# Column order of the moving operand in the fp32r products of a two-block forward pass

## The chip, the cores and the metric

The kernel runs on one core of a Trainium2 chip. The metric is the device time of one execution in microseconds (us), as the median of several runs. Engines are named as the profile names them: PE is the matrix engine (PEld its weight loads), DVE the vector engine, ACT the scalar engine, POOL and SP the two others.

## The reference

The program is the forward pass of two transformer-like blocks over 512 tokens of width 1,024, all in float32. The first block has a layer norm, a wide input projection, a spatial gating branch, a gated delta rule branch, a merge of the two, and a mixture of 32 experts (two chosen per token). The second block prepends 16 meta tokens and has attention with rotary positions, a gated linear recurrence, a merge, and a gated feed-forward part.

```
h = layer_norm(x)
proj = h @ w_in + b_in                               # all inputs of both mixers
merged = sigmoid(gate_a) * (y_a @ w_pa) + sigmoid(gate_b) * (y_b @ w_pb)
h = layer_norm(alpha * h + merged @ w_o)
h = layer_norm(alpha * h + moe(h))                   # 32 experts, top 2
proj = rmsnorm(h) @ w_in_2                           # q, k, v, rnn input, gates
h = h + (g_attn * attention + g_rnn * rnn) @ w_out
h = h + (silu(g) * u) @ w_ffn_out                    # g, u = rmsnorm(h) @ w_ffn_in
```

## The kernel before

Most products are made from split operands. `split` (L137) writes a float32 tile as two tiles of type fp32r: the high part is a copy on ACT, the low part is the rest, a subtraction on DVE. `mm3` (L162 to L166) then adds three matmuls into one PSUM bank: high by high (L164), high by low (L165), low by high (L166). Its second and third arguments are the stationary pair, loaded before each matmul; its fourth and fifth are the moving pair, whose columns run through the array.

The dense products come in two forms. `dense_fm` (L168) computes 128 output features for all 512 tokens: the stationary tiles are 128 columns of weights, the moving tiles are the tokens, 512 columns, with 8 steps over the width, so 24 matmuls into one bank. The projections of the first block (`gmlp`, `delta`), the gates of the second (`gates`) and the first half of the feed-forward part (`ffn`) use it; ACT, and in `ffn` also DVE, takes the bank out. `dense_tm`, `dense_tok` and `tm_step` compute 128 tokens by 512 features: the tokens are stationary and 512 columns of weights move. Weights come as float32 chunks by DMA on SP's queue (`wraw_load`, L156) and are split in `wchunk` (L148), in `split_w` (L307), `split_kv` (L1643) and `split_q` (L1739).

Five further places have moving fp32r tiles: `merge_b` (L810) moves 256 columns, two runs of 128; `rnn_x` (L1952) moves 264; the attention scores (L2053) move 264 columns of keys and the attention output (L2087) 512 columns of probabilities; the experts' results go back to the tokens in `add` (L1287 and L1288), 512 columns, and `add_res` (L1293) adds that bank to the residual on DVE. `combine` (L1295) does this 8 times for each of the 16 pairs of experts. `moe` gives the PSUM pool `psA` four buffers (L1158).

The expert products themselves (L1231 and L1261) are plain float32. Each is issued as two passes, and two experts stand side by side, 64 output rows each, in the two halves of the array. Rows of tokens for the experts are picked by fp32r products of 256 columns (L1194, L1195). Four small DVE operations are named below for their read patterns: in the routing of tokens L1031 multiplies the 32 expert logits of a token, taken from the four groups by turns (a step of 8), and L1004 forms 128 products in order; in `delta` L531 copies 32 columns of a PSUM bank and L582 reads 32 at an inner step of 32. Expert weights are loaded ahead in 1 MB chunks (`ahead`, L1123) on SP's queue.

The order of instructions on PE, and in some stretches on DVE and ACT too, is written out by hand (`manual_schedule` in `layer_in`, `moe`, `norm_kvq`, `block2` and `mix_out`); elsewhere a scheduler puts them in the order of the program.

Of the kernel before, what the change touches and what calls it, by code (L numbers as in the profile page):

```python
# [44 lines left out]
def weave(chain, others):  # L45

    for f in others:
        next(chain, None)
        f()
    for _ in chain:  # L50
        pass


class Net:
# [93 lines left out]
    def wchunk(self, wap, r0, nk, c0, ncol):  # L148

        raw = self.wraw_load(wap, r0, nk, c0, ncol)  # L150
        hi = self.whl.tile([128, nk, ncol], FR, name="whi")
        lo = self.whl.tile([128, nk, ncol], FR, name="wlo")
        self.split(hi, lo, raw)
        return hi, lo

# [124 lines left out]
    def layer_in(self, ctx, gp, v, hT):  # L280
# [24 lines left out]
        lo, ws = {}, []  # L305

        def split_w(n):  # L307
            hl = [self.whl.tile([128, 2, 512], FR, name=m) for m in ("whi", "wlo")]
            ws.append(hl)
            self.act(hl[0], raws[n], AF.Copy)  # L310
            return lambda: V.tensor_tensor(hl[1], raws[n], hl[0].bitcast(FT), OP.subtract)

        def stats(t):
            one = slice(t, t + 1)
# [115 lines left out]
    def gmlp(self, ctx, gp, v, hT):  # L430
        nc, I = self.nc, self.I
        w_in = I["w_in"][0]
        tp = self.pool(ctx, "gt", 2)
        lg = self.bcast(gp, I["gm_ln_g"], D, "gm_lg")
        lb = self.bcast(gp, I["gm_ln_b"], D, "gm_lb")
        bs = self.bcast(gp, I["gm_b_s"], D, "gm_bs")

        wT = gp.tile([128, NK, 128], FT, name="gm_wT")
        ws = gp.tile([128, NK, 128], FT, name="gm_ws")
        nc.sync.dma_start(ws, I["gm_w_s"][0].rearrange("g t s -> t g s"))  # L440
        for g0 in range(0, NK, 4):
# [12 lines left out]
        for g in range(NK):  # L454
            pu = self.dense_fm(w_in, g * 128, hT)
            u = tp.tile([128, S], FT, name="gm_u")
            self.act(u, pu, AF.Gelu, bias=self.vec[:, g:g + 1])
# [12 lines left out]
        for m in range(NK):  # L470
            pa = tp.tile([128, S], FT, name="gm_pa")
            self.act(pa, self.dense_fm(w_pa, m * 128, (yhi, ylo)), AF.Copy)
            nc.scalar.dma_start(self.pa_d[m], pa)

    def delta(self, dp, hT, vb):
# [13 lines left out]
        with ExitStack() as c:  # L489
# [166 lines left out]
        with ExitStack() as c:  # L656
# [119 lines left out]
            def gate(dst, c0, b0, func):  # L776

                for m in range(NK):
                    z = tp.tile([128, S], FT, name="zs")
                    self.act(z, self.dense_fm(w_in, c0 + m * 128, hT), func, bias=self.vec[:, b0 + m:b0 + m + 1])  # L780
                    nc.scalar.dma_start(dst[m], z)

            gate(self.zt_d, 5120, 40, AF.Silu)
# [13 lines left out]
    def merge_b(self, tp, yb, mhi, mlo):  # L797

        nc, I = self.nc, self.I
        for m in range(NK):  # L800
# [6 lines left out]
            pb = self.psA.tile([128, 512], FT, name="psA")  # L807
            for i, (yhi, ylo) in enumerate(yb):
                for k in range(NK):
                    self.mm3(pb[:, i * 256:(i + 1) * 256], hi[:, k, :], lo[:, k, :], yhi[:, :, k, :], ylo[:, :, k, :],  # L810
                             k == 0, k == NK - 1)
            nc.vector.tensor_tensor(sb, pb, sb, OP.mult)
# [342 lines left out]
    def moe(self, pctx):  # L1155
# [3 lines left out]
        with ExitStack() as ctx:  # L1159
# [121 lines left out]
            def add(part, t, half):  # L1281
# [2 lines left out]
                ps = self.psA.tile([128, 512], FT, name="psA")  # L1284
                cs = slice(half * 512, (half + 1) * 512)
                a = PT[:M, TOKS[t]]
                nc.tensor.matmul(ps, a, yhi[:M, cs], start=True, stop=False)  # L1287
                nc.tensor.matmul(ps, a, ylo[:M, cs], start=False, stop=True)  # L1288
                return lambda: add_res(ps, t, half)

            def add_res(ps, t, half):
                x = self.res[:, t, half * 512:(half + 1) * 512]
                nc.vector.tensor_tensor(x, x, ps, OP.add)  # L1293

            def combine(part, between=lambda: None):  # L1295
                for t in range(NT):
# [318 lines left out]
    def norm_kvq(self, c, h, xT, kv, gp):  # L1615
# [25 lines left out]
        xn, pk, ws, wq = {}, {}, [], []  # L1641

        def split_kv(n):  # L1643
            hl = [self.whl.tile([128, 2, 512], FR, name=m) for m in ("whi", "wlo")]
            ws.append(hl)
            self.act(hl[0], raws[n], AF.Copy)
            return lambda: V.tensor_tensor(hl[1], raws[n], hl[0].bitcast(FT), OP.subtract)

        def stats(t):

# [88 lines left out]
        def split_q(n):  # L1739
            raw = self.wraw_load(w_in, 2 * n * 128, 2, 0, 512)  # L1740
            out = []
            for j in range(2):
                hl = [gp.tile([128, 1, 512], FR, name=f"{m}{2 * n + j}") for m in ("ga", "rn")]
                r = raw[:, j:j + 1, :]
                self.act(hl[0], r, AF.Copy)
                out.append(lambda hl=hl, r=r: V.tensor_tensor(hl[1], r, hl[0].bitcast(FT), OP.subtract))
                wq.append(hl)
            return out

# [185 lines left out]
    def rnn_x(self, p, n, vec, xT):  # L1935
# [12 lines left out]
        for j in range(2):  # L1948
            js = slice(j * H, (j + 1) * H)
            ps = self.psA.tile([128, 512], FT, name="psA")  # L1950
            for k in range(NK):
                self.mm3(ps[:, :H], hi[:, k, :], lo[:, k, :], nhi[:, k, js], nlo[:, k, js], k == 0, k == NK - 1)  # L1952
            self.act(xr[:, 2 + j * H:2 + (j + 1) * H], ps[:, :H], AF.Copy)
# [27 lines left out]
    def gates(self, p, n, xT, rn, ga):  # L1981
# [7 lines left out]
        self.act(ga[n], ps, AF.Tanh, scale=0.5)  # L1989
        yield  # L1990
        g = rn[n]
        self.act(g, self.dense_fm(w_in, 4608 + n * 128, real), AF.Tanh, scale=0.5)
        yield
        ps = self.dense_fm(w_in, 2560 + n * 128, real)
        x = p.tile([128, S], FT, name="grx")
        self.act(x, ps, AF.Copy)
        y = p.tile([128, S], FT, name="gry")
        self.act(y, ps, AF.Square)
# [37 lines left out]
    def attention(self, tp, h, kv, rn, ga, gp, mix):  # L2036
# [11 lines left out]
        def weights(t):  # L2048
            tok = TOKS[t]
            ps = self.psD.tile([128, 2, 512], FT, name="psD")  # L2050
            for j in range(2):
                js = slice(j * H, (j + 1) * H)
                self.mm3(ps[:, j, :H], q[0][:, tok], q[1][:, tok], khi[:, g, js], klo[:, g, js], True, True)  # L2053
            m = tp.tile([128, 1], FT, name="m", bufs=4)
            nc.vector.tensor_reduce(m, ps[:, :, :H], AX.XY, OP.max)
            nc.vector.scalar_tensor_tensor(m, m, -1.0, qs[:, t, h:h + 1], op0=OP.mult, op1=OP.mult)
            pr = tp.tile([128, 2, H], FT, name="pr", bufs=3)
            s = tp.tile([128, 1], FT, name="s", bufs=4)
            self.act(pr, ps[:, :, :H], AF.Exp, bias=m, scale=qs[:, t, h:h + 1], accum_out=s)
# [24 lines left out]
        vs = slice(g * 128, (g + 1) * 128)  # L2084
        for b in range(NT + 1):
            M = 128 if b else META
            self.mm3(po, vhi[:M, b, vs], vlo[:M, b, vs], Phi[:M, b, :], Plo[:M, b, :], b == 0, b == NT)  # L2087
        o = tp.tile([128, S], FT, name="ao")
        nc.vector.scalar_tensor_tensor(o, ga[h], 1.0, po, op0=OP.add, op1=OP.mult)
        yield  # L2090
        nc.vector.tensor_tensor(o, o, rn[h], OP.add)
        self.dbg("mix%d" % h, o)
# [57 lines left out]
    def ffn(self, ctx, h, hT, first):  # L2150
# [3 lines left out]
        fp = self.pool(ctx, "ffp", side="right")  # L2154
        f = (fp.tile([128, NF, S], FR, name="f_hi"), fp.tile([128, NF, S], FR, name="f_lo"))
        for m in range(NF):
            pg = self.dense_fm(w_i, m * 128, hT) if m else first[0]
            g = tp.tile([128, S], FT, name="fg")
            self.act(g, pg, AF.Silu)
            pu = self.dense_fm(w_i, (NF + m) * 128, hT) if m else first[1]  # L2160
            nc.vector.tensor_tensor(g, g, pu, OP.mult)
# [99 lines left out]
```

## Time and profile before

| what | value |
|---|---|
| median of 3 runs | 2016.44 us (2016.29 to 2017.75) |
| the profiled execution | 2013.71 us |
| its span | 2011.2 us |
| PE busy | 1931.3 us (96%), 9,833 matmuls |
| PEld, DVE, ACT busy | 1402.6 us, 1002.4 us, 700.1 us |
| moved by DMA | 362.22 MB |

The span is that of the instructions of one profiled execution; its time is 2.5 us longer, and the median of the runs is 2.7 us above that time. A matmul's listed duration has a modelled end and overlaps the next matmul; the distance from one start to the next is what a matmul takes in a row of them. A line number can be that of a helper: L68 is every ACT operation, L140 every low part, L164 to L166 every split product.

### The profile page before, as it was taken

To read this page: it belongs to the slowest core of one execution; us is meant where nothing else is said; L and a number is where in the kernel's file an instruction comes from. 1 tells how busy PE (TensorE), PEld (TensorE's weight loads), DVE (VectorE), ACT (ScalarE), POOL (GpSimd) and SP (SyncE) were. 2 spreads that over 40 slices of the span, in tenths; PEclk is the share of its full clock that TensorE was granted. 3 is DMA by queue.
4 is the path that set the end of the run, shared out by engine and by line. 5 is a ranking of instruction groups with operands and counts; after the bars stand their busy time and mean duration, and the time that the engine had idled before them with its cause. 6 is when DMAs were issued, how large, how long until landed. Compare 5 with 4: busy or idle time off the path is not lost.

```text
span 2011.2 us, 24965 instructions
## 1 busy us (share of the span) xinstructions
PE 1931.3 (96%) x9833; PEld 1402.6 (70%) x9833; DVE 1002.4 (50%) x1908; ACT 700.1 (35%) x1220; POOL 3.1 (0%) x12
## 2 busy tenths in 40 slices
PE   7999999879999899999999989999999999999999
PEld 5787668668888754554435536888888788888887
DVE  6833667744555822322223249557878753333222
ACT  5232434323332321111101116357677632222211
POOL 0000000000000000000000000000000000000000
PEclk9999999989999899999999998999999999999999
DMA  8423433464378499996999983432221333333231
GB/s 257 104 84 97 115 71 85 132 146 85 91 247 291 155 349 402 409 409 269 405 409 410 407 309 130 126 90 79 79 59 53 99 106 94 93 95 93 93 115 62
DMA packets 309015, 362.22 MB, mean 180 GB/s; under 512 B 29921, under 2 KB 196354, under 8 KB 308770
## 3 DMA queue, kind: packets, MB, share of 16 engines
q1 hardware_dynamic: 301986, 345.94, 51.8%
q10 hardware_dynamic: 6912, 14.68, 1.9%
q8 instruction: 78, 1.28, 0.3%
q14 instruction: 39, 0.32, 0.0%
HBM read 340.64 MB, written 19.94 MB: 179 GB/s over the span
## 4 chain that ended last, share of the span: by engine, by line
PE 45%; DMA 4%; DVE 2%; ACT 1%; issue 0%; SPq 0%; ACTq 0%; DVEq 0%
PE psA L165 10%; PE psA L164 10%; PE psA L166 10%; PE psB L1231 3%; DMA mwt<-in_w 3%; PE psB L1261 2%; PE psD L1975 1%; PE psA L1287 1%; PE psA L1288 1%; PE psD L164 1%; PE psB L2073 1%; PE psA L1195 1%; PE psA L1194 1%; PE psB L164 1%; PE psD L166 0%; PE psD L165 0%
## 5 line engine op out<-in xcount | busy, mean ns | idle before, releaser
L68 ACT ACTIVATE whi<-raw 128x1024 fp32r<-128x1024 f32 (+1 forms) x203 | 213.4, 1055 | 530.5 <-PE psA L165 300.7
L140 DVE TENSOR_TENSOR wlo<-raw,whi 128x1024 fp32r<-128x1024 f32 (+1 forms) x195 | 236.7, 1215 | 293.6 <-ACT whi L68 276.5
L1231 PE MATMUL psB<-mwt,XT 128*64 128x512 f32 x1008 | 226.1, 597 | 3.0 <-DVEq L1345 2.1
L166 PE MATMUL psA<-hT_hi,wlo 128*128 128x512 f32 (+1 forms) x456 | 184.7, 405 | 12.9 <-DVE wlo L140 12.9
L164 PE MATMUL psA<-hT_hi,whi 128*128 128x512 f32 (+1 forms) x456 | 185.7, 407 | 0.9 <-ACT whi L68 0.9
L165 PE MATMUL psA<-hT_lo,whi 128*128 128x512 f32 (+1 forms) x456 | 185.6, 407 | 0.0
L1231 PEld LDWEIGHTS psB<-mwt,XT 128*64 128x64 f32 x1008 | 73.3, 138 | 142.3 <-issue 136.4
L165 PE MATMUL psA<-hn_lo,whi 128*128 128x512 f32 (+1 forms) x368 | 141.8, 385 | 0.3 <-DVE hn_lo L2125 0.3
L164 PE MATMUL psA<-hn_hi,whi 128*128 128x512 f32 (+1 forms) x368 | 141.9, 386 | 0.2 <-ACT hn_hi L68 0.2
L166 PE MATMUL psA<-hn_hi,wlo 128*128 128x512 f32 (+1 forms) x368 | 141.7, 385 | 0.0
L1293 DVE TENSOR_TENSOR res<-res,psA 128x512 f32<-128x512 f32 x128 | 79.5, 681 | 103.0 <-PE psA L1288 103.0
L1237 DVE TENSOR_TENSOR sl<-sl,psB 128x512 f32<-128x512 f32 x16 | 11.0, 688 | 233.7 <-PE psB L1231 233.7
L1261 PE MATMUL psB<-mwt,hbT 128*64 128x512 f32 x480 | 110.2, 593 | 5.2 <-DMA mwt<-in_w 5.2
L164 PE MATMUL psA<-xn_hi,whi 128*128 128x512 f32 (+1 forms) x320 | 113.1, 353 | 0.4 <-ACT qx L68 0.4
L165 PE MATMUL psA<-xn_lo,whi 128*128 128x512 f32 (+1 forms) x320 | 112.3, 351 | 0.0
L166 PE MATMUL psA<-xn_hi,wlo 128*128 128x512 f32 (+1 forms) x320 | 111.9, 350 | 0.0
L166 PEld LDWEIGHTS psA<-hT_hi,wlo 128*128 128x128 f32 (+1 forms) x456 | 86.6, 190 | 35.3 <-DVE wlo L140 13.9
L165 PEld LDWEIGHTS psA<-hT_lo,whi 128*128 128x128 f32 (+1 forms) x456 | 86.5, 190 | 26.9 <-issue 7.5
L164 PEld LDWEIGHTS psA<-hT_hi,whi 128*128 128x128 f32 (+1 forms) x456 | 86.8, 190 | 24.5 <-issue 3.4
L1261 PEld LDWEIGHTS psB<-mwt,hbT 128*64 128x64 f32 x480 | 35.9, 137 | 76.5 <-issue 63.7
L68 ACT ACTIVATE hbT<-psA 128x512 f32<-128x512 f32 x16 | 9.6, 598 | 213.3 <-PE psA L1245 213.3
L165 PEld LDWEIGHTS psA<-hn_lo,whi 128*128 128x128 f32 x368 | 69.2, 188 | 15.7 <-DVE hn_lo L2125 0.5
(570 smaller groups left out, 3714.1 us busy)
## 6 DMA issues: line engine op xcount, KB each, us to landing
mwt<-in_w SPq DMA_DIRECT2D x188, 1024.0 KB, 13.6
raw<-in_w_in SPq DMA_DIRECT2D x108, 512.0 KB, 7.1
raw<-in_w_ffn_in SPq DMA_DIRECT2D x44, 512.0 KB, 3.9
raw<-in_w_ffn_out SPq DMA_DIRECT2D x22, 512.0 KB, 3.6
raw<-in_w_pa SPq DMA_DIRECT2D x8, 512.0 KB, 3.7
raw<-in_w_pb SPq DMA_DIRECT2D x8, 512.0 KB, 5.7
raw<-in_w_o SPq DMA_DIRECT2D x8, 512.0 KB, 6.7
raw<-in_w_out SPq DMA_DIRECT2D x8, 512.0 KB, 3.6
```

What stands on the lines that cost most here:

```text
L68: ins = self.nc.scalar.activation(out, in_, func, **kw)
L140: self.nc.vector.tensor_tensor(lo, x, hi.bitcast(FT), OP.subtract)
L164: nc.tensor.matmul(out, whi, xhi, start=first, stop=False)
L165: nc.tensor.matmul(out, whi, xlo, start=False, stop=False)
L166: nc.tensor.matmul(out, wlo, xhi, start=False, stop=last)
L1194: nc.tensor.matmul(ps[:, :n], h1hi[:, k, TOKS[t]], P[:, t, :], start=(t == 0), stop=False)
L1195: nc.tensor.matmul(ps[:, :n], h1lo[:, k, TOKS[t]], P[:, t, :], start=False, stop=(t == NT - 1))
L1231: nc.tensor.matmul(ps[CAP * i:CAP * (i + 1), :], XT[:, r0 + k, x0 + CAP * i:x0 + CAP * (i + 1)], w_, start=(r0 + k == 0), stop=(r0 + k == ...
L1261: nc.tensor.matmul(pys[half][CAP * i:CAP * (i + 1), :], hT[:, r0 + k, CAP * i:CAP * (i + 1)], ws[i][:, k, half * 512:(half + 1) * 512], st ...
L1287: nc.tensor.matmul(ps, a, yhi[:M, cs], start=True, stop=False)
L1288: nc.tensor.matmul(ps, a, ylo[:M, cs], start=False, stop=True)
L1293: nc.vector.tensor_tensor(x, x, ps, OP.add)
```

## The change

A moving tile of the fp32r products named above is read with its two halves by turns: column 0 of the first half, column 0 of the second half, column 1 of the first, and so on. The matmul writes its PSUM bank from column 0 to the last without gaps, as before.

Where tokens, keys, probabilities or expert results move, the bank then holds the results by turns, and the ACT or DVE instruction that takes the bank out reads every second column of it (`unturned`) and writes two contiguous halves (`halves`). Where weights move, the split itself reads every second column of the float32 chunk and writes the even columns into the first half of the tile and the odd ones into the second; read by turns, they come in their natural order, and the bank needs nothing. This holds for chunks of 512 columns; chunks of 128 columns are stationary and stay as they are.

Unchanged are the expert products, the picking of rows (L1194, L1195), the product of L496, and the first two banks of the feed-forward part, which `mix_out` computes in two parts of 256 columns (L2146). The numbers of instructions, DMAs, tiles and bytes stay the same, and so does their order.

```diff
+def halves(x):
+    return x.rearrange("p (s c) -> p s c", s=2)
+def by_turns(x):
+    return x.rearrange("p (s c) -> p c s", s=2)
+def unturned(x):
+    return x.rearrange("p (c s) -> p s c", s=2)
+def split_views(hi, lo, raw):
+    st = [z.rearrange("p k (s c) -> p k s c", s=2) for z in (hi, lo)]
+    return st, raw.rearrange("p k (c s) -> p k s c", s=2), [z.rearrange("p k (s c) -> p k c s", s=2) for z in (hi, lo)]
...
 def wchunk(self, wap, r0, nk, c0, ncol):
+        if ncol == 512:
+            st, raw, hl = split_views(hi, lo, raw)
+            self.split(*st, raw)
+            return hl
         self.split(hi, lo, raw)
...
 def dense_fm(self, wap, c0, xT):
-            self.mm3(ps, hi[:, k, :], lo[:, k, :], xhi[:, k, :], xlo[:, k, :], k == 0, k == NK - 1)
-        return ps
+            self.mm3(ps, hi[:, k, :], lo[:, k, :], by_turns(xhi[:, k, :]), by_turns(xlo[:, k, :]), k == 0, k == NK - 1)
+        return unturned(ps)
...
-                self.act(xc[:, 3:], pq, AF.Identity, bias=self.vec[:, 16 + m:17 + m])
+                self.act(halves(xc[:, 3:]), pq, AF.Identity, bias=self.vec[:, 16 + m:17 + m])
...
-                nc.tensor.matmul(ps, a, yhi[:M, cs], start=True, stop=False)
-                nc.tensor.matmul(ps, a, ylo[:M, cs], start=False, stop=True)
+                nc.tensor.matmul(ps, a, by_turns(yhi[:M, cs]), start=True, stop=False)
+                nc.tensor.matmul(ps, a, by_turns(ylo[:M, cs]), start=False, stop=True)
...
-                x = self.res[:, t, half * 512:(half + 1) * 512]
-                nc.vector.tensor_tensor(x, x, ps, OP.add)
+                x = halves(self.res[:, t, half * 512:(half + 1) * 512])
+                nc.vector.tensor_tensor(x, x, unturned(ps), OP.add)
...
-                self.mm3(ps[:, j, :H], q[0][:, tok], q[1][:, tok], khi[:, g, js], klo[:, g, js], True, True)
+                self.mm3(ps[:, j, :H], q[0][:, tok], q[1][:, tok], by_turns(khi[:, g, js]), by_turns(klo[:, g, js]), True, True)
...
-            pg = self.dense_fm(w_i, m * 128, hT) if m else first[0]
+            pg = self.dense_fm(w_i, m * 128, hT) if m else halves(first[0])
-            self.act(g, pg, AF.Silu)
+            self.act(halves(g), pg, AF.Silu)
...
```

The places left out have the same two forms: `split_views` in `split_w`, `split_kv` and `split_q`; `by_turns` with `unturned` and `halves` in `gmlp`, `gate`, `merge_b`, `rnn_x`, `gates`, the exponent of `attention` and its output.

## Rows read from the trace of the kernel before

**Rows 1.** The page, part 2: busy tenths of PE, granted clock and DMA in 40 slices

```profile
PE   7999999879999899999999989999999999999999
...
PEclk9999999989999899999999998999999999999999
DMA  8423433464378499996999983432221333333231
```

**Rows 2.** Timeline of PE in the feed-forward part: start, us, engine, line, operation

```profile
1799.88 0.40 PE L166 MATMUL psA<-hn_hi,wlo 128*128 128x512 f32 x1
...
1802.91 0.39 PE L164 MATMUL psA<-hn_hi,whi 128*128 128x512 f32 x1
```

**Rows 3.** Timeline of PE in the merge (256 columns) and the attention scores (264 columns)

```profile
604.80 0.28 PE L166 MATMUL psA<-at,wlo 128*128 128x256 f32 x1
...
606.96 0.28 PE L166 MATMUL psA<-at,wlo 128*128 128x256 f32 x1
...
1314.27 0.28 PE L165 MATMUL psD<-kTlo,qhi 128*128 128x264 f32 x1
...
1314.88 0.40 PE L164 MATMUL psA<-xn_hi,whi 128*128 128x512 f32 x1
```

**Rows 4.** Timeline of PE in the expert stage: plain float32 passes, two side by side

```profile
1032.95 13.93 PE L1231 MATMUL psB<-mwt,XT 128*64 128x512 f32 x64
1046.72 0.59 PE L1261 MATMUL psB<-mwt,hbT 128*64 128x512 f32 x1
```

**Rows 5.** L164 in the whole span: stretch, its length, PE busy and count, clock, DMA

```profile
0.00:2011.20 2011.20, 708.29 (x1864) 351.90 (x1864) 0.99 0.54 180
```

**Rows 6.** Groups by line and form, PE: count, busy us, mean ns, idle before

```profile
L164 PE MATMUL psA<-xn_hi,whi 128*128 128x264 f32 x128 | 36.5, 285 | 0.4 <-ACT qx L68 0.4
...
L164 PE MATMUL psA<-at,whi 128*128 128x256 f32 x128 | 36.2, 283 | 0.0
...
L164 PE MATMUL psD<-kThi,qhi 128*128 128x264 f32 x64 | 19.9, 311 | 1.4 <-DVE PTlo L140 1.4
...
L164 PE MATMUL psA<-hn_hi,whi 128*128 128x256 f32 x32 | 9.0, 283 | 0.2 <-ACT hn_hi L68 0.2
...
L164 PE MATMUL psA<-hT_hi,whi 128*16 128x512 f32 x8 | 3.2, 395 | 0.9 <-ACT whi L68 0.9
```

**Rows 7.** L164 in five stretches, columns as in rows 5

```profile
0.00:90.00 90.00, 20.58 (x50) 9.61 (x50) 0.97 0.68 179
...
330.00:460.00 130.00, 49.42 (x119) 23.49 (x119) 0.93 0.53 129
...
700.00:1198.00 498.00, 0.00 (x0) 0.00 (x0) 0.99 0.98 381
1198.00:1310.00 112.00, 42.90 (x112) 21.06 (x112) 0.94 0.42 138
...
1570.00:1645.00 75.00, 38.05 (x102) 19.18 (x102) 1.00 0.35 106
```

**Rows 8.** The page, part 5: the splits of weights on ACT and DVE

```profile
L68 ACT ACTIVATE whi<-raw 128x1024 fp32r<-128x1024 f32 (+1 forms) x203 | 213.4, 1055 | 530.5 <-PE psA L165 300.7
L140 DVE TENSOR_TENSOR wlo<-raw,whi 128x1024 fp32r<-128x1024 f32 (+1 forms) x195 | 236.7, 1215 | 293.6 <-ACT whi L68 276.5
```

**Rows 9.** One line of DVE each: ns min/median/max, first and last start, forms

```profile
L1031 DVE TENSOR_TENSOR XT<-logit,ro_oh x1: 378/378/378, 691.8 to 691.8; 128x128 f32<-128x128 f32 x1
...
L1004 DVE TENSOR_TENSOR XT<-ro_oh x2: 283/287/291, 694.0 to 695.0; 128x128 f32<-128x128 f32 x2
...
L582 DVE TENSOR_SCALAR dcol<-psB x1: 191/191/191, 300.2 to 300.2; 128x32 f32<-128x32 f32 x1
...
L531 DVE COPY dcol<-psB x1: 193/193/193, 197.4 to 197.4; 128x32 f32<-128x32 f32 x1
```

**Rows 10.** Timeline of DVE in the expert stage: seven additions of one combine

```profile
1056.51 4.28 DVE L1293 TENSOR_TENSOR res<-res,psA 128x512 f32<-128x512 f32 x7 [8.80 <-PE psA L1288]
```

More of the change, by code (lines that the diff above doesn't have):

```diff
@@ L307, in split_w @@
         def split_w(n):
-            hl = [self.whl.tile([128, 2, 512], FR, name=m) for m in ("whi", "wlo")]
+            st, r, hl = split_views(*(self.whl.tile([128, 2, 512], FR, name=m) for m in ("whi", "wlo")), raws[n])
             ws.append(hl)
-            self.act(hl[0], raws[n], AF.Copy)
-            return lambda: V.tensor_tensor(hl[1], raws[n], hl[0].bitcast(FT), OP.subtract)
+            self.act(st[0], r, AF.Copy)
+            return lambda: V.tensor_tensor(st[1], r, st[0].bitcast(FT), OP.subtract)
         def stats(t):
@@ L456, in gmlp @@
             u = tp.tile([128, S], FT, name="gm_u")
-            self.act(u, pu, AF.Gelu, bias=self.vec[:, g:g + 1])
+            self.act(halves(u), pu, AF.Gelu, bias=self.vec[:, g:g + 1])
             ps = self.psB.tile([128, 512], FT, name="psB")
@@ L471, in gmlp @@
             pa = tp.tile([128, S], FT, name="gm_pa")
-            self.act(pa, self.dense_fm(w_pa, m * 128, (yhi, ylo)), AF.Copy)
+            self.act(halves(pa), self.dense_fm(w_pa, m * 128, (yhi, ylo)), AF.Copy)
             nc.scalar.dma_start(self.pa_d[m], pa)
@@ L779, in gate @@
                     z = tp.tile([128, S], FT, name="zs")
-                    self.act(z, self.dense_fm(w_in, c0 + m * 128, hT), func, bias=self.vec[:, b0 + m:b0 + m + 1])
+                    self.act(halves(z), self.dense_fm(w_in, c0 + m * 128, hT), func, bias=self.vec[:, b0 + m:b0 + m + 1])
                     nc.scalar.dma_start(dst[m], z)
@@ L809, in merge_b @@
                 for k in range(NK):
-                    self.mm3(pb[:, i * 256:(i + 1) * 256], hi[:, k, :], lo[:, k, :], yhi[:, :, k, :], ylo[:, :, k, :],
+                    self.mm3(pb[:, i * 256:(i + 1) * 256], hi[:, k, :], lo[:, k, :],
+                             *(y[:, :, k, :].rearrange("p s c -> p c s") for y in (yhi, ylo)),
                              k == 0, k == NK - 1)
-            nc.vector.tensor_tensor(sb, pb, sb, OP.mult)
+            sb4 = sb.rearrange("p (i s c) -> p i s c", i=2, s=2)
+            nc.vector.tensor_tensor(sb4, pb.rearrange("p (i c s) -> p i s c", i=2, s=2), sb4, OP.mult)
             nc.vector.tensor_tensor(pa, pa, sb, OP.add)
@@ L1643, in split_kv @@
         def split_kv(n):
-            hl = [self.whl.tile([128, 2, 512], FR, name=m) for m in ("whi", "wlo")]
+            st, r, hl = split_views(*(self.whl.tile([128, 2, 512], FR, name=m) for m in ("whi", "wlo")), raws[n])
             ws.append(hl)
-            self.act(hl[0], raws[n], AF.Copy)
-            return lambda: V.tensor_tensor(hl[1], raws[n], hl[0].bitcast(FT), OP.subtract)
+            self.act(st[0], r, AF.Copy)
+            return lambda: V.tensor_tensor(st[1], r, st[0].bitcast(FT), OP.subtract)
         def stats(t):
@@ L1742, in split_q @@
             for j in range(2):
[L1743 to L1746, printed above, removed]
+                st, r, hl = split_views(*(gp.tile([128, 1, 512], FR, name=f"{m}{2 * n + j}") for m in ("ga", "rn")),
+                                        raw[:, j:j + 1, :])
+                self.act(st[0], r, AF.Copy)
+                out.append(lambda st=st, r=r: V.tensor_tensor(st[1], r, st[0].bitcast(FT), OP.subtract))
                 wq.append(hl)
@@ L1951, in rnn_x @@
             for k in range(NK):
-                self.mm3(ps[:, :H], hi[:, k, :], lo[:, k, :], nhi[:, k, js], nlo[:, k, js], k == 0, k == NK - 1)
-            self.act(xr[:, 2 + j * H:2 + (j + 1) * H], ps[:, :H], AF.Copy)
+                self.mm3(ps[:, :H], hi[:, k, :], lo[:, k, :], by_turns(nhi[:, k, js]), by_turns(nlo[:, k, js]),
+                         k == 0, k == NK - 1)
+            self.act(halves(xr[:, 2 + j * H:2 + (j + 1) * H]), unturned(ps[:, :H]), AF.Copy)
         c = p.tile([128, T], FT, name="xc")
@@ L1988, in gates @@
         yield
-        self.act(ga[n], ps, AF.Tanh, scale=0.5)
+        self.act(halves(ga[n]), ps, AF.Tanh, scale=0.5)
         yield
         g = rn[n]
-        self.act(g, self.dense_fm(w_in, 4608 + n * 128, real), AF.Tanh, scale=0.5)
+        self.act(halves(g), self.dense_fm(w_in, 4608 + n * 128, real), AF.Tanh, scale=0.5)
         yield
@@ L1995, in gates @@
         x = p.tile([128, S], FT, name="grx")
-        self.act(x, ps, AF.Copy)
+        self.act(halves(x), ps, AF.Copy)
         y = p.tile([128, S], FT, name="gry")
-        self.act(y, ps, AF.Square)
+        self.act(halves(y), ps, AF.Square)
         yield
@@ L2058, in weights @@
             s = tp.tile([128, 1], FT, name="s", bufs=4)
-            self.act(pr, ps[:, :, :H], AF.Exp, bias=m, scale=qs[:, t, h:h + 1], accum_out=s)
+            self.act(pr.rearrange("p a (s c) -> p a s c", s=2), ps[:, :, :H].rearrange("p a (c s) -> p a s c", s=2), AF.Exp, bias=m,
+                     scale=qs[:, t, h:h + 1], accum_out=s)
             nc.vector.reciprocal(s, s)
@@ L2086, in attention @@
             M = 128 if b else META
-            self.mm3(po, vhi[:M, b, vs], vlo[:M, b, vs], Phi[:M, b, :], Plo[:M, b, :], b == 0, b == NT)
+            self.mm3(po, vhi[:M, b, vs], vlo[:M, b, vs], by_turns(Phi[:M, b, :]), by_turns(Plo[:M, b, :]), b == 0, b == NT)
         o = tp.tile([128, S], FT, name="ao")
-        nc.vector.scalar_tensor_tensor(o, ga[h], 1.0, po, op0=OP.add, op1=OP.mult)
+        nc.vector.scalar_tensor_tensor(halves(o), halves(ga[h]), 1.0, unturned(po), op0=OP.add, op1=OP.mult)
         yield
@@ L2156, in ffn @@
         for m in range(NF):
-            pg = self.dense_fm(w_i, m * 128, hT) if m else first[0]
+            pg = self.dense_fm(w_i, m * 128, hT) if m else halves(first[0])
             g = tp.tile([128, S], FT, name="fg")
-            self.act(g, pg, AF.Silu)
-            pu = self.dense_fm(w_i, (NF + m) * 128, hT) if m else first[1]
-            nc.vector.tensor_tensor(g, g, pu, OP.mult)
+            self.act(halves(g), pg, AF.Silu)
+            pu = self.dense_fm(w_i, (NF + m) * 128, hT) if m else halves(first[1])
+            nc.vector.tensor_tensor(halves(g), halves(g), pu, OP.mult)
             self.split(f[0][:, m, :], f[1][:, m, :], g)
```

## Prediction

> **What bounds the kernel.** I read the slices of the page first. [...] DMA is at nine tenths only in the slices of the experts. So outside the expert stage the time is the sum of PE's matmuls, and the question is what one matmul takes in a row of them. The timeline answers it by the distance of starts. In the feed-forward part 14 matmuls of 512 columns start between 1799.88 and 1802.91 us, 13 steps, so one takes 233.1 ns [rows 2]. [...] The forms with fewer columns: 256 columns take 2.16 us / 18 = 120 ns, 264 take 0.61 us / 5 = 122 ns [rows 3]. [...]
>
> The plain float32 passes show the contrast. Their 64 records stand two and two side by side, so 13.77 us hold 32 steps of 430.3 ns [rows 4]. [...]
>
> **The change, part by part.**
>
> *The moving read.* [...] No row before shows such a read on PE. [...] I take 16.2.
>
> *How many.* L164 has 1,864 matmuls [rows 5]. Of these 128 + 64 are changed ones with 264 columns and 128 with 256; 32 with 256 and 8 for the 16 columns of L496 stay as they are [rows 6]. That leaves 1,504 with 512 columns. L165 and L166 have the same numbers. So 4,512 x 16.2 ns = 73.1 us, 576 x 8.4 = 4.8 us, 384 x 9.7 = 3.7 us, together 81.6 us. The 96 and 24 matmuls that the code issues one by one in the two hand-ordered norms (L348, L352, L1707 to L1716) I leave out.
>
> *What is not on the path.* In four stretches PE idles between its matmuls: the first 90 us, the delta rule, the start of the second block and the end of attention. They hold 50 + 119 + 112 + 102 = 383 of the 1,864, a fifth [rows 7]. There a chain through DVE, ACT or DMA sets part of the end, and a faster matmul waits longer for it. I count half of their share, so 81.6 x 0.205 / 2 = 8.4 us are lost.
>
> *The expert stage.* Its changed matmuls are L1287 and L1288. DMA is at 0.98 of its engines there [rows 7], and the additions that empty their banks go back to back at 4.28 / 7 = 0.61 us, longer than the two matmuls of 0.23 each [rows 10]. A gain there is worth nothing to me, and at most 256 x 16.2 ns = 4.1 us.
>
> *The splits of weights* read every second column. ACT takes 1,055 ns and DVE 1,215 for one [rows 8]. Below nothing I exclude, since the element count stays. Above, the nearest strided row: DVE takes 378 ns for 128 elements that lie 8 apart, read from four groups by turns, and 287 ns for 128 in order [rows 9], so 0.71 ns more for an element, 730 ns for 1,024. A step of two is nearer to order than a step of eight, so I take nothing. The cover: before these ACT operations ACT sat idle for 530.5 us, waiting for PE [rows 8], and a chunk of 512 columns serves 24 matmuls, 5.2 us, against 1.8 us on ACT and 1.9 on DVE at the bound. Were the cover gone, some 50 chunks would cost at most 36 us.
>
> *Taking results out of PSUM* with a step of two. DVE reads 32 elements of a bank at a step of 32 in 191 ns and 32 in order in 193 [rows 9], so nothing; the bound above is again 0.71 ns an element, 364 ns for a bank. ACT and DVE are off the path in the dense stretches, with four buffers for the banks. Only the additions of the experts could show it (a rival below). Writing two contiguous halves, and the views themselves, add no instruction and no DMA; no wait is added and nothing moves in a queue. Next to be late, where PE gets faster, are the softmax steps on ACT and DVE in attention, which is busy there but not full.
>
> **Sum.** 81.6 - 8.4 = 73.2 us off the profiled execution's 2013.71 gives 1940.5; the median of the runs is 2.7 us above that execution, so I predict 1943. [...]
>
> **Rivals.**
>
> *A: the new order is what costs.* Place: every changed matmul. The strided row of DVE is by turns too, four groups 8 elements apart, and pays 0.71 ns an element [rows 9]. [...] At DVE's 0.71 ns it is 364 ns x 4,512 and about 185 ns x 960, 1,820 us, so 3,840. It decides from any price over 0.035 ns a column, since then the 16.2 ns are spent. Against it: PE already takes a column in 0.455 ns where DVE's split takes 1.19 [rows 2, 8], so its reader is not DVE's; and the matmuls on two separate runs of 128 columns [rows 3] lose little more than those on one. For it: the only read by turns in the trace is slow. I give it 0.22. [...]
>
> *B: the loss is not a matter of order.* It could come from a clock between PE and its operands, or from the product of fp32r itself; then the change doesn't do what it says, and the time stays at 2016, give or take 4. For it: 120 ns at 256 columns and 233 at 512 are nearly the same rate, whatever the stretch. [...] 0.08.
>
> *C: part of the gain is given back at the experts' additions.* If each L1293 takes 364 ns more, 128 of them are 47 us; they go back to back [rows 10], the pool has four banks, and the next product waits for one. 1943 + 47 = 1990. The rows of PSUM speak against it. Half a gain in the matmuls, 1980, falls into the same class. 0.12.
>
> **The numbers.** The forecast has 0.58, A 0.22, C 0.12, B 0.08. The predicted time is the forecast's. Its own range is 1920 to 1967: with all over one column a cycle (19.8 ns, 13.3 at 256, 12 at 264) 101 us are saved, 91 without the four stretches' half share, and 4 us more in the expert stage, 1921; at two thirds of the forecast's gain it is 1967. The range asked for takes in C and B: 1920 to 2022; A lies far outside. This kernel's measurement can tell about 0.2%, 4 us, from no change. Faster: the forecast and C, 0.70. Within 0.2%: most of B, 0.06. Slower: A and the rest of B, 0.24.
>
> **What would show it.** Right: starts 217 ns apart in the feed-forward part, 110 to 114 for 256 and 264 columns; float32 passes still 430 per step; L1293 still 0.61 us apart; the expert stage as long as before. Wrong: starts at 233 (B), at 430 or more (A), L1293 near 0.97 us apart and PE waiting for it (C), or splits of weights so long that PE waits for `whi` or `wlo` in the feed-forward part's second half.

## The result and the profile after

The changed kernel takes 1964.57 us (median of 4 runs, 1959.66 to 1965.80), the kernel before 2016.37 beside it: a ratio of 0.9741, 95% interval 0.972 to 0.9762. That is 52 us, where 73 were forecast; the time lies in the forecast's own range (1920 to 1967), near its upper end. The profiled execution took 1959.66 us, its span 1957.5, 53.7 less than before.

Three lines of the page, part 2, after (PE, its granted clock, DMA, in 40 slices), beside [rows 1]:

```profile
PE   6899999879999899999899997999999999999999
...
PEclk9999999989999899999999998999999999999999
...
DMA  8433434464378499997999994332221243333331
```

PE is still what is busy: 1849.1 of 1957.5 us (94%) by the page, part 1. Now the timeline of PE after: the feed-forward part (19 steps between the first two rows), the merge's 256 columns (18 steps), the scores' 264 columns (8 steps), and two plain float32 rows of the expert stage.

```profile
1749.84 0.38 PE L191 MATMUL psA<-hn_lo,whi 128*128 128x512 f32 x1
...
1753.94 0.38 PE L192 MATMUL psA<-hn_hi,wlo 128*128 128x512 f32 x1
...
590.26 0.28 PE L192 MATMUL psA<-at,wlo 128*128 128x256 f32 x1
...
592.27 0.28 PE L192 MATMUL psA<-at,wlo 128*128 128x256 f32 x1
...
1396.71 0.28 PE L190 MATMUL psD<-kThi,qhi 128*128 128x264 f32 x1
...
1397.62 0.28 PE L192 MATMUL psD<-kThi,qlo 128*128 128x264 f32 x1
...
1012.36 13.93 PE L1259 MATMUL psB<-mwt,XT 128*64 128x512 f32 x64
1026.12 4.54 PE L1289 MATMUL psB<-mwt,hbT 128*64 128x512 f32 x18
```

A matmul of 512 columns went from 233.1 ns [rows 2] to 4.10 us / 19 = 215.8, one of 256 from 120 [rows 3] to 112, one of 264 from 122 to about 113 (0.91 us / 8 by these rows, 112.5 in the mean over all). The float32 passes stand as they did, 13.76 us for 32 steps [rows 4]. Half a float32 pass of 512 columns is 430.3 / 2 = 215.2 ns by [rows 4]: read in order, a matmul took 17.9 ns more than that, by turns it takes 0.6 more.

The splits of weights and the experts' additions after (page, part 5, and the timeline of DVE), beside [rows 8, 10]:

```profile
L90 ACT ACTIVATE whi<-raw 128x1024 fp32r<-128x1024 f32 (+1 forms) x203 | 234.9, 1162 | 462.6 <-PE psA L191 289.0
L162 DVE TENSOR_TENSOR wlo<-raw,whi 128x1024 fp32r<-128x1024 f32 (+1 forms) x195 | 248.4, 1275 | 251.1 <-ACT whi L90 232.5
```

```profile
1006.67 4.28 DVE L1321 TENSOR_TENSOR res<-res,psA 128x512 f32<-128x512 f32 x7 [6.71 <-PE psA L1316]
```

Taking a bank out of PSUM with a step of two costs DVE nothing here: seven additions in 4.28 us as before [rows 10]. The mean over all splits rose by 107 ns on ACT and 60 on DVE; most of them are contiguous, so those of step two rose by more (below). And PE waits more, by its list of waits (us in total, times, longest). The first line is before's; for `rg` at the scores before has no line. The other two are after's:

```profile
PE psA L166 <- DVE wlo L140: 12.9, 2, 7.5
...
PE psA L192 <- DVE wlo L162: 18.5, 6, 10.0
...
PE psD L190 <- ACT rg L90: 5.4, 6, 1.0
```

**Where the gain went.** PE issues the same 9,833 matmuls in the same order in every kernel here that keeps all the work, and ACT and DVE run theirs in one and the same order in before and after. So the start of one and the same matmul can be compared from kernel to kernel. To be had: the changed matmuls that start in a stretch of before, times 17.5, 9.5 or 8 ns for 512, 264 or 256 columns (means over all). The last three columns are kernels of the experiments below (one profiled execution each, us won). The granted clock, 0.986 over the whole span before and 0.985 after, is not behind the loss as a whole, but it differs from stretch to stretch and moves single entries by 2 us or more.

| stretch of before, us | to be had | after | order at PSUM | high part on DVE | both |
|---|---|---|---|---|---|
| 0-100, norm and first products | 5.0 | 0.8 | -1.1 | 0.2 | 0.9 |
| 100-330, gating, projections | 14.6 | 10.8 | 8.5 | 11.3 | 9.2 |
| 330-560, delta rule | 9.1 | 3.6 | 3.0 | 4.3 | 2.4 |
| 560-700, merge | 8.0 | 4.0 | 5.6 | 4.6 | 5.9 |
| 700-1198, experts | 4.3 | 1.5 | 2.2 | 0.8 | 0.6 |
| 1198-1310, second block's start | 6.1 | -0.2 | 0.8 | 1.5 | 1.2 |
| 1310-1570, attention and recurrence | 16.0 | 7.5 | 7.6 | 11.5 | 11.5 |
| 1570-1645, end of attention | 4.2 | -0.9 | 1.2 | -1.3 | 1.5 |
| 1645-2012, feed-forward | 26.9 | 26.7 | 26.9 | 26.7 | 26.9 |
| sum | 94.2 | 53.8 | 54.7 | 59.6 | 60.1 |

The feed-forward part paid in full. Of 94 us, 40 were lost, nearly all of it before 1645 us.

### The profile page after: what moved, and what is told of

The parts are those of the page before. It is cut to its first block, busy times and chain, and to the rows that moved or that the text cites. A ratio compares the mean times of both kernels' runs of the same rounds, so it can differ in the third digit from the quotient of the medians.

```text
span 1957.5 us, 24980 instructions
## 1 busy us (share of the span) xinstructions
PE 1849.1 (94%) x9833; PEld 1397.6 (71%) x9833; DVE 1012.6 (52%) x1908; ACT 722.0 (37%) x1220; POOL 3.1 (0%) x12
## 4 chain that ended last, share of the span: by engine, by line
PE 34%; DVE 8%; ACT 6%; DMA 4%; issue 1%; SPq 0%; ACTq 0%; DVEq 0%
PE psA L191 7%; PE psA L190 7%; PE psA L192 7%; PE psB L1259 4%; DMA mwt<-in_w 3%; PE psB L1289 2%; DVE wlo L162 1%; PE psA L1315 1%; DVE th L2059 1%; ACT whi L90 1%; PE psA L1316 1%; ACT th L90 1%; DVE xc L1986 1%; ACT pr L90 1%; ACT L90 1%
## 5 line engine op out<-in xcount | busy, mean ns | idle before, releaser
L90 ACT ACTIVATE whi<-raw 128x1024 fp32r<-128x1024 f32 (+1 forms) x203 | 234.9, 1162 | 462.6 <-PE psA L191 289.0
L162 DVE TENSOR_TENSOR wlo<-raw,whi 128x1024 fp32r<-128x1024 f32 (+1 forms) x195 | 248.4, 1275 | 251.1 <-ACT whi L90 232.5
L192 PE MATMUL psA<-hT_hi,wlo 128*128 128x512 f32 (+1 forms) x456 | 177.5, 390 | 16.2 <-DVE wlo L162 16.2
L190 PE MATMUL psA<-hT_hi,whi 128*128 128x512 f32 (+1 forms) x456 | 178.4, 391 | 0.9 <-ACT whi L90 0.9
L191 PE MATMUL psA<-hT_lo,whi 128*128 128x512 f32 (+1 forms) x456 | 178.3, 391 | 0.0
L190 PE MATMUL psA<-hn_hi,whi 128*128 128x512 f32 (+1 forms) x368 | 136.5, 371 | 0.2 <-ACT hn_hi L90 0.2
L191 PE MATMUL psA<-hn_lo,whi 128*128 128x512 f32 (+1 forms) x368 | 136.4, 371 | 0.3 <-DVE hn_lo L2155 0.3
L192 PE MATMUL psA<-hn_hi,wlo 128*128 128x512 f32 (+1 forms) x368 | 136.3, 370 | 0.0
L191 PE MATMUL psA<-xn_lo,whi 128*128 128x512 f32 (+1 forms) x320 | 108.1, 338 | 0.0
```

Source lines behind the costliest of these rows:

```text
L90: ins = self.nc.scalar.activation(out, in_, func, **kw)
L162: self.nc.vector.tensor_tensor(lo, x, hi.bitcast(FT), OP.subtract)
L190: nc.tensor.matmul(out, whi, xhi, start=first, stop=False)
L191: nc.tensor.matmul(out, whi, xlo, start=False, stop=False)
L192: nc.tensor.matmul(out, wlo, xhi, start=False, stop=last)
```

## Experiments

Three theories of the loss: T1, in attention ACT's and DVE's work on a head now sets the pace; T2, the split of step two makes chunks of weights late; T3, the stretches are bound by something that the change does not touch.

### The change in two parts, and a third form of it

Tokens only: `wchunk`, `split_w`, `split_kv` and `split_q` as in before.

```diff
-        if ncol == 512:
-            st, raw, hl = split_views(hi, lo, raw)
-            self.split(*st, raw)
-            return hl
```

> The change without its weights: products whose moving operand is a tile of tokens read it by turns, weights are split and read in order as before. Counted from the trace of after: 1,080 x 3 matmuls of 512 columns, 576 of 264 and 384 of 256 keep the gain (65 us at 17.5, 9.5 and 8 ns each), 1,392 lose it (24 us). Theory T2 (the split that reads every second column delays chunks in 0-100, 560-700, 1198-1310 and 1570-1645 us): what is lost is mostly the second half of the feed-forward part, 528 x 17.5 ns = 9.2 us, and about 4 us come back where the long split held PE; about 1970 us, ratio 0.977. Theory T3 (those stretches are bound by something else, and the long split costs nothing): about 1974 to 1978 us, ratio 0.980 or a little over. Both: starts 215.8 ns apart in the first half of the feed-forward part, 233 in the second; ACT's whi from raw 1,055 to 1,065 ns everywhere.

Measured: 1969.93 us (1966.49 to 1971.80), ratio 0.9771, interval 0.9755 to 0.9786. T2's number. The stretch 597 to 611 us, 2.9 us longer than before in after, is 0.5 shorter here. Of the 2.9, 1.7 us go with the granted clock: 0.90 over the 16.8 us that the stretch takes in after, 1.00 in before and here.

Weights only: before, with the lines that the first left out.

> The other part alone: the kernel before with the weights of 512 columns stored even columns first, so that they are read by turns; tokens are read in order. T2: 9 us won in the second half of the feed-forward part, a few where weights are the moving operand elsewhere, and 3 to 5 us lost where chunks come late (around 600 us and 1570-1645 us): 2008 to 2012 us, ratio 0.996 to 0.998. T3: nothing is lost, up to 15 us won: 2001 to 2005, ratio 0.993. Both: ACT's split of 128x1024 takes 1,531 ns where it reads every second column and 1,060 where it doesn't; with PE's starts 215.8 apart in the second half of the feed-forward part, 233 in the first.

Measured: 2004.27 us (1999.74 to 2006.81), ratio 0.9939, interval 0.9924 to 0.9954: 10.8 us won, T3's number, not T2's. In its trace 9.2 us are won in the second half of the feed-forward part and 4 between 611 and 700 us, and 3.4 are lost between 1600 and 1645. T2 had named the second of these only as "a few". But the 3.4 us are what the granted clock makes of that stretch (0.93 over 48.3 us, 1.00 before), and over 2 of the 4 go with the clock too (0.93 before, 0.96 here). So this run does not show that late chunks cost anything. The two parts add up to 45.1 + 10.8 = 55.9 us, about what both do together (52).

Order at PSUM: weights are split and stored in order and read by turns, and their results are put in order where they are taken out. This holds at every such place but the query product, which is read in order; two of the places are `dense_tok` and `mix_out`:

```diff
+                self.mm3(ps[:M], xhi, xlo, by_turns(hi[:, k % 2, :]), by_turns(lo[:, k % 2, :]), k == 0, k == n - 1)
+            yield unturned(ps)
...
-                V.tensor_tensor(x[:, 512:], x[:, 512:], ps, OP.add)
+                V.tensor_tensor(halved(x[:, 512:]), halved(x[:, 512:]), ps, OP.add)
```

> After, but weights are split and stored in order, and read by turns all the same; their results lie in PSUM by turns and are put in order by the instruction that takes them out (the query product alone is left in order). T2: the whole of after's gain and what the long splits cost on top: 1950 to 1957 us, ratio to before 0.967 to 0.971, and PE's loss around 597-611 us gone. T3: as after, 1963 to 1966, ratio 0.974. If reading PSUM with a step of two did cost DVE something on the path, it would be slower than after. Both: ACT's whi from raw 1,055 to 1,065 ns everywhere, DVE's wlo near 1,225.

Measured: 1957.95 us (1957.67 to 1959.72), ratio 0.9714, interval 0.97 to 0.9728, against 0.972 to 0.9762 for after: some 5 us better by the ratios, though the intervals just touch; a little less than T2's number and outside T3's. The split on its page, part 5:

```profile
L95 ACT ACTIVATE whi<-raw 128x1024 fp32r<-128x1024 f32 (+1 forms) x203 | 213.1, 1054 | 484.4 <-PE psA L192 299.6
```

It is back at before's 1,055 ns [rows 8]. By matmul starts, after's losses at 597-611 us (+2.9) and 1600-1645 (+2.8) become -1.0 and +0.9. With the clock put aside (1.7 us in the first of after's, 0.96 in the second of both kernels) some 2 us are the edit's in each. Two more pairs below differ by the same edit, by 6.7 us (with the mix on POOL) and by 1.4 (with the copy on DVE). So T2 holds, for some 5 of the 40 us. (In 0-100 and 190-220 us this execution had a granted clock of 0.91 and 0.89, after 0.97 and 1.00; the difference of some 2 us in each goes with the clock.)

### Which orders are fast, and what a step costs a split

After, with ten orders of the moving tile in the feed-forward part's first half and four steps of the split in its second.

```diff
+FMO = ["halves"] + [n for n in ORD for _ in range(2)] + ["halves"]
+STEPS = [2, 1, 4, 8] * 3
...
+            pg = self.dense_fm(w_i, m * 128, hT, order) if m else halves(first[0])
...
+            pss = self.dense_tm(w_o, half * 512, f, nk=NF, by=STEPS)
```

> After with two measurements in the feed-forward part. First half: the moving tile is read in ten orders, two m (96 matmuls) each: in order; by turns from 2, 4 and 8 equal parts; all even columns, then all odd; by turns from the halves, but two or four neighbours at a time; and by turns from two neighbouring runs of 2, 4 or 16 columns. M1 (a column costs more when its neighbour has just been read): 233 ns in order, 215.8 for 2, 4, 8 parts and for runs of 16, about 224 for pairs and 229 for fours, and even/odd 215.8 or 233 as two columns' distance is far enough or not. M2 (each of two far places delivers every second cycle): 215.8 for the parts alone, 233 for all neighbouring runs. M3 (any order that isn't one straight run is fetched in another way): 215.8 for all but the first. Second half: the split of weights reads with a step of 2, 1, 4, 8 in turn, chunk by chunk. S1 (paid by how many elements of what is fetched together are used): 1,060, 1,531 and more, up to about 2,400, for ACT at steps 1, 2, 4, equal at 4 and 8. S2 (any step costs the same): 1,531 for 2, 4 and 8. The kernel's own time says nothing here.

Stretches of PE, one for each order in the sequence of the expectation (start to end, length, PE busy and matmuls, clock, DMA). PE is busy throughout, so length over count is close to what one takes; matmuls cut by the edges are counted too, so it comes out some 2% low.

```profile
1623.00:1645.00 22.00, 22.00 (x96) 1.00 0.40 118
1645.30:1666.00 20.70, 20.70 (x98) 1.00 0.34 100
1666.00:1693.00 27.00, 27.00 (x97) 1.00 0.27 80
1693.20:1740.00 46.80, 46.80 (x97) 1.00 0.15 45
1740.30:1783.00 42.70, 42.70 (x96) 1.00 0.17 49
1783.80:1815.00 31.20, 31.20 (x97) 1.00 0.24 68
1815.20:1839.00 23.80, 23.80 (x96) 1.00 0.30 89
1839.40:1861.00 21.60, 21.60 (x94) 1.00 0.31 91
1861.80:1882.00 20.20, 20.20 (x95) 1.00 0.32 93
1882.50:1903.00 20.50, 20.50 (x96) 1.00 0.32 102
```

By the starts of neighbouring matmuls, one took:

| order of columns | ns |
|---|---|
| in order | 233 |
| by turns from 2, 4, 8 equal parts | 216, 283, 491 |
| even columns, then odd | 453 |
| halves by turns, two, four at a time | 327, 252 |
| two neighbouring runs of 2, 4, 16 by turns | 233, 216, 216 |

None of the three theories holds. M1 and M3 wanted 216 for four and eight parts, M2 wanted 233 for runs of 4 and 16. What the rows do show: 216 ns was reached by single columns from two places by turns, 4, 16 or 256 columns apart. From two places 2 columns apart it was 233, as in order; four and eight places (283, 491), two or four columns at a time (327, 252) and even columns before odd (453) took longer than in order. Why, no run shows.

The split, on the timeline of ACT (start, us), chunks of step 4, 8, 2 and 1, in this order (the steps stand in the trace's operands):

```profile
1948.21 2.06 ACT L114 ACTIVATE whi<-raw 128x1024 fp32r<-128x1024 f32 x1 [4.12 <-PE psA L216]
1953.81 2.11 ACT L114 ACTIVATE whi<-raw 128x1024 fp32r<-128x1024 f32 x1 [3.54 <-PE psA L216]
1960.61 1.20 ACT L114 ACTIVATE whi<-raw 128x1024 fp32r<-128x1024 f32 x1 [4.69 <-PE psA L216]
1972.39 1.06 ACT L114 ACTIVATE whi<-raw 128x1024 fp32r<-128x1024 f32 x1 [10.58 <-PE psA L216]
```

Steps 4 and 8 cost alike, 2.06 and 2.11 us, twice the contiguous 1.06: S1's numbers, not S2's. But step 2 took 1.20 us here, where PE was reading eight parts by turns (ACT's next copy, which waits for them, starts 11.78 us later, 24 times 491 ns), not the 1.53 that it takes in after's second half, and that was not expected.

### Why the split of step two is slow in after

The weights of the second feed-forward product are stored as in after; the second 512 result columns read them in order.

```diff
+            if as_stored:
+                hi, lo = (z.rearrange("p k c s -> p k s c") for z in (hi, lo))
...
+                    nc.vector.tensor_tensor(unturned(o), halves(pss[t]), unturned(h[:, t, cs]), OP.add)
```

> After, with the weights of the feed-forward part's second product still stored even columns first by a split of step 2; the first 512 columns of the result read them by turns, as after, the second 512 read them as they are stored (the result is put in order where it leaves PSUM). C1 (a split of step 2 is slowed where PE reads by turns at the same time): first half as after, about 1,530 ns on ACT and 1,530 on DVE, second half 1,126 and 1,222 as in the few places where PE read in order in the kernel with weights alone. C2 (what slows it is the place or the size of these chunks, not PE): 1,530 in both halves. PE: 215.8 ns in the first half, 233 in the second, 264 matmuls and 4.5 us more than after: 1967 to 1970 us.

Groups by form in two windows, 1841 to 1898 us (PE reads by turns) and 1899 to 1955 us (PE reads in order); count, busy us, mean ns:

```profile
L90 ACT ACTIVATE whi<-raw 128x1024 fp32r<-128x1024 f32 x11 | 17.3, 1573 | 38.8 <-PE psA L192 32.4 <-issue 3.4 <-PE psA L191 3.1
L162 DVE TENSOR_TENSOR wlo<-raw,whi 128x1024 fp32r<-128x1024 f32 x11 | 17.0, 1542 | 36.6 <-ACT whi L90 36.6
...
L162 DVE TENSOR_TENSOR wlo<-raw,whi 128x1024 fp32r<-128x1024 f32 x10 | 12.3, 1226 | 39.9 <-ACT whi L90 39.9
L90 ACT ACTIVATE whi<-raw 128x1024 fp32r<-128x1024 f32 x10 | 11.3, 1134 | 43.8 <-PE psA L192 43.8
```

C1: the same instruction, on the same chunks, takes 1,573 ns while PE reads by turns and 1,134 while PE reads in order; on DVE 1,542 and 1,226. A contiguous split does not suffer: in order at PSUM it takes 1,054 ns beside the same PE. PE shows no loss in return, 215.8 ns in after. So what costs is a split of step two beside PE's reads by turns, and ACT (439 ns) and DVE (316 ns) pay. In the one execution, of 1966.85 us, 4.6 us of after's gain are given back in the second 512 columns, as expected.

### Attention

In a head of after, the timeline of DVE, ACT and PE:

```profile
1394.29 0.67 DVE L2121 TENSOR_TENSOR ao<-ao,rn 128x512 f32<-128x512 f32 x1
...
1395.00 0.63 ACT L90 ACTIVATE ga<-ao 128x512 fp32r<-128x512 f32 x1 [0.89 <-DVE xr L1975]
...
1395.54 0.69 ACT L90 ACTIVATE rg<-psD,vec 128x528 f32<-128x528 f32 x1
...
1396.27 0.38 PE L190 MATMUL psD<-kThi,qhi 128*128 128x264 f32 x1 [0.95 <-ACT rg L90]
```

ACT stands at `ga<-ao`, the high part of a head's mix, until DVE's addition (L2121) is done at 1394.96; its row names a DVE instruction of 0.06 us right behind that one. The second of a head's two sigmoids `rg` is queued behind it, and PE's scores wait for the buffer that `rg` empties. Only DVE's low part follows on `ga`; PE needs it at the end of attention.

Two of the four taps of the convolution left out:

```diff
-        for j in range(1, 4):
+        for j in range(3, 4):
```

> After, with two of the four taps of the convolution left out (two DVE instructions of 0.75 us for each head, ahead of the scan on DVE); the output is another one. T1 (ACT's copy ga<-ao waits for DVE's chain, and the sigmoid behind it): the copy comes 1.5 us earlier, PE's wait for rg goes, 6 to 8 us less than after: 1957 to 1959. Rival (ACT alone, or PE's own order, sets the distance from head to head): the wait stays, 1963 to 1965, as after.

Measured: 1973.33 us (1973.13 to 1975.02), 9 us more than after with less to do. Neither theory had that. The order of ACT and DVE in this stretch is a scheduler's, and with two instructions fewer it put the copy ahead of the table load and of both sigmoids `rg`, where in after it stands between the two: the timeline of ACT, and PE's wait.

```profile
1395.96 0.63 ACT L90 ACTIVATE ga<-ao 128x512 fp32r<-128x512 f32 x1 [4.23 <-DVE ao L2121]
1396.61 1.28 ACT L90 ACT_TABLE_LOAD   x1
1397.91 0.70 ACT L90 ACTIVATE rg<-psD,vec 128x528 f32<-128x528 f32 x1
```

```profile
PE psD L2004 <- ACT rg L90: 13.7, 6, 2.4
```

So it is no test of DVE's load, but rather one of the copy's place: it waits 4.23 us for DVE with `rg` behind it, and PE waits 13.7 us in six heads. DVE's order changed too, so what the copy alone costs is not shown by this run.

The mix's last addition and its split on POOL:

```diff
+            nc.gpsimd.tensor_tensor(o, o, rn[h], OP.add)
+            nc.gpsimd.tensor_copy(mix[h][0], o)
+            nc.gpsimd.tensor_tensor(mix[h][1], o, mix[h][0].bitcast(FT), OP.subtract)
```

> After, with the last addition of each head's mix and its split (one addition and one subtraction on DVE, one copy on ACT) put on POOL, which is idle; the last head's stay where they were. ACT's and DVE's other instructions keep their order, PE's order is the same. T1 (in attention ACT holds the sigmoid rg, for which PE's scores wait, behind the copy ga<-ao, which waits for the end of DVE's chain): the wait of PE's psD for ACT's rg, 5.4 us in six waits in after, is gone, the distance from head to head falls from 34.69 to about 33.8 us, 1957 to 1959 us, ratio to before 0.971. Rival T1b (the loop of a head through DVE and ACT is as long as that whatever stands in ACT's queue): another wait of PE takes its place, 1962 to 1965. Rival T1c: POOL's instructions slow DVE's down: DVE's scan, 1.19 us now, and its splits longer, 1965 or more.

> The kernel that puts the weights' results in order where they leave PSUM, with the mix on POOL as well. The two gains lie in different stretches; T1: 1951 to 1953 us, ratio to before 0.968, faster than both kernels. T1b: as without the move, 1957 to 1959. T1c: slower than that.

Measured: 1962.57 us (1959.47 to 1968.05), ratio 0.9749, interval 0.9732 to 0.9766, as after; with the order at PSUM 1955.84, ratio 0.9712, as without POOL (0.9714). The wait for `rg` is gone, but heads are 34.8 us apart (34.7 in after), and the transposes now wait for the softmax. POOL and DVE in the timeline:

```profile
1395.92 1.27 POOL L2125 TENSOR_TENSOR rn<-ao,ga 128x512 fp32r<-128x512 f32 x1
...
1396.16 2.15 DVE L2007 TENSOR_TENSOR ig<-ig,xc 128x1056 f32<-128x1056 f32 x1 [1.79 <-ACT ig L90]
```

DVE's product took 2.15 us in this head, with POOL's subtraction beside it, and 1.26 in after: what ACT's queue gave, POOL took. That is T1c, at another instruction than it named. T1b, in whose range the first time lies, was not excluded by this.

The copy alone, on DVE:

```diff
-        self.split(*mix[h], o)
+            nc.vector.tensor_copy(mix[h][0], o)
+            nc.vector.tensor_tensor(mix[h][1], o, mix[h][0].bitcast(FT), OP.subtract)
```

> After, with the copy ga<-ao of each head's mix (the last head's apart) done by DVE in place of ACT, between the addition before it and the subtraction behind it. The order of all else stays. On DVE it falls into the 0.68 us in which DVE waited for ACT's copy. T1 with T1c (ACT's queue is what holds the scores; with the mix on POOL the gain was eaten because DVE's product ig took 2.15 us beside POOL's subtraction in place of 1.26): PE's wait for rg gone, ig at 1.26 us, the transposes' wait for pr small, about 33.8 us from head to head, 5 to 6 us less than after: 1958 to 1960. T1b (a loop through DVE and ACT of that length, whatever stands in ACT's queue): the transposes wait for pr as they did with the mix on POOL, 1962 to 1965, as after.

> The kernel that puts the weights' results in order where they leave PSUM, with the same copy on DVE. T1 with T1c: 5 to 6 us less than without it, 1950 to 1953, ratio to before 0.968, the fastest of all. T1b: 1956 to 1959.

Measured: 1954.60 us (1953.67 to 1957.47), ratio 0.9696, interval 0.9682 to 0.9709; with the order at PSUM 1953.21 (1949.15 to 1955.54), ratio 0.968, interval 0.9665 to 0.9696. (Before took 2017.48 us beside these two, so the ratios compare better than the times.) The first is faster than even T1 with T1c had it. In its timeline:

```profile
1391.46 0.70 ACT L90 ACTIVATE rg<-psD,vec 128x528 f32<-128x528 f32 x1 [0.36 <-PE psD L2004]
...
1391.91 0.43 DVE L2126 CAST ga<-ao 128x512 fp32r<-128x512 f32 x1
...
1392.22 0.38 PE L190 MATMUL psD<-kThi,qhi 128*128 128x264 f32 x1
...
1393.09 1.26 DVE L2007 TENSOR_TENSOR ig<-ig,xc 128x1056 f32<-128x1056 f32 x1
```

`rg` runs as soon as PE has filled its bank, the scores wait for nothing, `ig` is at 1.26 us, and heads are 33.94 us apart: T1 with T1c, and T1b falls. In the table, 4 us come back in attention. The medians fall by more than that; runs of one kernel lie 4 to 6 us apart, so no more than the 4 us is read as the edit's. Both kernels lie below after's interval; which of the two is faster these intervals do not tell.

### What stays lost

With both edits 34 of 94 us remain unwon. One place can be read from after, T3: at 428.74 us PE had waited 10.03 us for `wlo` of a chunk (7.46 before, the longest wait for a split in either), because ACT waited for the chunk itself. The first line is before's; the others are after's PE, ACT and SP's queue.

```profile
442.02 0.79 PE L166 MATMUL psA<-hT_hi,wlo 128*128 128x512 f32 x1 [7.46 <-DVE wlo L140]
...
428.74 0.80 PE L192 MATMUL psA<-hT_hi,wlo 128*128 128x512 f32 x1 [10.03 <-DVE wlo L162]
...
415.84 1.06 ACT L90 ACTIVATE whi<-raw 128x1024 fp32r<-128x1024 f32 x1 [6.98 <-DMA raw<-in_w_in]
...
427.36 1.06 ACT L90 ACTIVATE whi<-raw 128x1024 fp32r<-128x1024 f32 x1 [9.35 <-DMA raw<-in_w_in]
...
406.68 8.60 SPq L678 DMA_DIRECT2D Xd<-Xs  x1
...
415.86 0.63 SPq L185 DMA_DIRECT2D raw<-in_w_in  x1
```

ACT's two waits there were 4.84 and 8.36 us before (the row of the second names a DVE instruction, but there too the copy starts when the chunk has landed). PE arrives 15.9 us earlier than before, the second copy starts only 13.8 us earlier. The rows of SP's queue show why the chunk is late in both kernels: its transfer is issued behind that of `Xd<-Xs`, whose issue takes 8.60 us (8.82 before). No run moved this issue, so that is read and not shown. The longer wait accounts for 2.6 us; for the other 31 no cause was tried.

## Why the prediction came out as it did

**The moving read**: right in kind, a little low in size. The terms of its sum, 16.2, 9.7 and 8.4 ns, and those of its range, 19.8, 13.3 and 12, were the author's estimates and no run shows them. By the rows 17.3 ns were saved at 512 columns (17.5 in the mean over all), 8 at 256 and 9 at 264, and no order that was run took less than 216 ns for 512. Two halves by turns beat reading in order, 215.8 ns against 233.1; more parts did not, four take 283 ns and eight 491.

**How many**: right; with the larger saving of each and the hand-ordered norms that it left out, some 90 us outside the expert stage in place of 81.6.

**What is not on the path** is the step that failed. It counted half of the share of four stretches, 8.4 us. Those four (with their edges in the table) kept 3.3 of 24.4 us, so about seven eighths was lost, 21 us. And attention from 1310 to 1570 us, taken at full gain as "busy there but not full", kept 7.5 of 16.0; gating and merge lost 4 each. The text had named the softmax steps on ACT and DVE as next to be late. The engines were right; the place that the runs show, for 4 us, was a copy in ACT's queue.

That the time still lies in the forecast's range owes something to luck: some 13 us more were to be had than it counted, and 32 more were lost. With its own 81.6 us and 40 lost the time would have been about 1975, outside the range.

**The splits of weights** were taken at nothing. Against a contiguous split of 1,054 ns, step two costs ACT 0.08 ns an element beside PE's reads in order (1,134) and 0.5 beside its reads by turns (1,573), inside the bound of 0.71. The cover, ACT's idle time, was there in the feed-forward part and missing in the merge and at the end of attention, where PE waited for `wlo`; the cost of some 5 us was within the 36 allowed.

**PSUM, the expert stage**: right, 0.61 us an addition as before, and 1.5 of 4.3 us won there.

**The rivals**: A fell, every changed form of matmul is faster (215.8 ns for 233.1, 112 for 120, 113 for 122); a read whose next element lies elsewhere did pay in ACT's split (steps 4 and 8 at 2.06 and 2.11 us, 1.06 in order) and in PE's even-then-odd read (453 ns for 233), but not from two places by turns (216). B, by which the loss (17.9 ns over half a float32 pass) is no matter of order, fell with the first two rows: 215.8. C's place was wrong; its idea, that a part is given back, came true elsewhere, and at 1964.57 the result lies between the forecast and C's half gain. A's threshold is 16.2 / 512 = 0.032 ns a column, not 0.035; nothing hangs on it.

## What to carry to other kernels

Price a faster engine stretch by stretch: where a row of its instructions was unbroken it won all here (26.7 of 26.9 us in the feed-forward part), where another engine's queue or a DMA ended waits it won an eighth in four stretches (3.3 of 24.4 us) and about half in attention (7.5 of 16.0), and half was too kind a guess. Look in the next engine's queue for an instruction that nobody needs soon and that waits for somebody slow: here `rg` waited behind a copy that waited 0.89 us for DVE in the head shown, and moving that copy was worth 4 us, about what all the strided splits cost. Where a reordered operand has to be put right, try it where the result leaves PSUM rather than by a strided read of SBUF beside a matmul; that was the faster of the two in two pairs of kernels here (ratios 0.9714 against 0.9741, 0.9712 against 0.9749) and not told apart in the third (0.968 against 0.9696).

## What was not expected of the hardware

- A read of step two took ACT 1,134 ns beside PE's reads in order and 1,573 beside its reads by turns from two halves, DVE 1,226 and 1,542. Beside PE's reads by turns from eight parts it took 1,200 on ACT.
- The order of a moving fp32r operand spans 216 to 491 ns for the same 512 columns; two runs only 4 columns apart serve as well as two halves (216 ns each).
- A product on DVE took 2.15 us beside POOL's subtraction, 1.26 without it. DVE's loss (0.89 us) is close to what was left of POOL's instruction when DVE's began (1.03); what the two share, no row shows.
